# A hybrid decoder step on one core: the first stage in a written order, its x loads on two other queues, and the final norm's sums through a ones matrix

## The chip, the core and the metric

The kernel runs on 1 core of one Trainium2 chip. The core has TensorE (PE in the rows; its weight loads are PEld), VectorE (DVE), ScalarE (ACT), GpSimd (POOL) and SyncE (SP). SP, ACT and POOL also issue DMAs; in the rows an issue stands under SPq, ACTq or POOLq. The metric is the device time of one execution in microseconds (us), as the median over runs.

## The reference

One inference step of one layer over 264 tokens (256 of a prompt, 8 single-token samples), width 2048, all in fp32. RMSNorm comes first, again ahead of the MLP, and once more at the end, where this change touches it:

```python
def rmsnorm(x, g):
    y = x * lax.rsqrt(jnp.mean(x * x, axis=-1, keepdims=True) + EPS)
    return y * g

hx = rmsnorm(x, norm_mix)
proj = hx @ w_in                      # 2048 -> 11264, split into nine parts
...                                   # short convolution branch, gated recurrence branch
x = x + mix @ w_out
h2 = rmsnorm(x, norm_ffn)
x = x + jnp.square(jax.nn.relu(h2 @ w_up)) @ w_down
y = rmsnorm(x, norm_final)
```

## The kernel before

Activations lie transposed: 128 partitions hold one block of 128 features, the free dimension the T = 264 tokens, and a width of 2048 is 16 such blocks (k = 0 to 15). Each product is made of three passes. A weight is split into a rounded part `whi` (a copy on ACT) and the rest `wlo` (a subtraction on DVE), an activation block into `xgh` (ACT, which multiplies by the norm's gain) and `xgl` (DVE), and TensorE adds wh·xh, wh·xl and wl·xh. The factor 1/rms of a norm is applied after the product.

**First stage** (lines 137 to 188). Its output blocks are the four of `HEAD`, accumulated in the four PSUM tiles `hd0` to `hd3`. Weights `w_hd` and input x come in four groups g of four blocks k: `wt0` and `xt0` in four single pieces, the other groups in halves of two blocks (512 KB of weights, 264 KB of x). Per block there are 12 matmuls of 264 columns (line 179). Per group ACT squares the x tile and DVE adds it to `xsq`; after the last group DVE folds that to `ss1` (lines 186 and 187). No order is written here: a scheduler sets each engine's order, and the loads stand in a high-priority block. SP issues weights and x of groups 1 to 3 in turn (lines 155 and 156).

The split tiles come from the pool `wsp` with four buffers a tag, so the ninth `whi` tile takes the buffer of the fifth, and its copy waits until TensorE has used that one. The first stage takes eight such tiles. The next two belong to `w`, the first weight tile of the projection loop (`fetch` and `half`, lines 476 to 482): their first user is `proj`, and their copies wait for the tiles of blocks 8 and 9, and of blocks 10 and 11.

**After it** (lines 484 to 527, in a block whose order is written): `sumsq` puts the squares' sums of 88 tokens at a time on partitions with three matmuls of one column, `rstd_diag` makes 1/rms there (DVE, DVE, ACT, DVE) and `rstd_bcast` spreads it back with one matmul. On TensorE `sumsq(ps1, ss1)` stands between the last `hd` matmul and the first `proj` one.

**The end** (lines 617 to 652). The last norm takes the same way: `sumsq` of `ss3` ahead of the last `dn` product, `sumsq` of the last block's squares behind it, `rstd_diag`, `rstd_bcast`, then DVE multiplies six pieces of the output and SP stores each. Behind `rstd_bcast` stand 48 matmuls of the tile `probe`, whose results nothing reads. At the very start ten matmuls `wps` on a ones tile keep TensorE busy while the first loads run.

Of the kernel before, what the change touches and what calls it, by code (L numbers as in the profile page):

```python
# [40 lines left out]
def hybrid_step(ctx: ExitStack, tc: tile.TileContext, x, par, sconv, shg, w_hd, w_in, w_br, w_out, w_up, w_dn,  # L41
# [115 lines left out]
    for g in range(4):  # L157
        xt, w = xts[g], wts[g]
        whi = [wsp.tile([P, 2, 512], F32R, tag="hi", name="whi") for _ in range(2)]
        wlo = [wsp.tile([P, 2, 512], F32R, tag="lo", name="wlo") for _ in range(2)]  # L160
        for j in range(4):
            k = 4 * g + j
            gk = pt[:, C_NMIX + k:C_NMIX + k + 1]
            hi = act.tile([P, T], F32R, tag="xg", name=f"xgh{k}")
            lo = act.tile([P, T], F32R, tag="xg", name=f"xgl{k}")
            wh, wl = whi[j // 2][:, j % 2], wlo[j // 2][:, j % 2]
            if g == 0:
                (nc.vector.tensor_copy if k == 0 else nc.scalar.copy)(wh, w[:, j])
                nc.scalar.activation(hi, xt[:, j], AF.Copy, scale=gk)
                nc.vector.tensor_tensor(wl, w[:, j], wh.bitcast(F32), op=ALU.subtract)  # L170
            else:
                if j % 2 == 0:
                    split(w[:, j:j + 2], whi[j // 2], wlo[j // 2])
                nc.scalar.activation(hi, xt[:, j], AF.Copy, scale=gk)
            nc.vector.scalar_tensor_tensor(lo, xt[:, j], gk, hi.bitcast(F32), op0=ALU.mult, op1=ALU.subtract)
            xg.append((hi, lo))
            for a, b, st, sp in ((wh, hi, k == 0, False), (wl, hi, False, False), (wh, lo, False, k == NK - 1)):
                for i in range(4):
                    nc.tensor.matmul(hps[i], a[:, i * P:(i + 1) * P], b, start=st, stop=sp)  # L179
        if g == 0:  # L180
            nc.scalar.activation(xsq, xt, AF.Square)
        else:
            sq = xp.tile([P, 4, T], F32, tag="xsq2", name="sq", bufs=2)
            nc.scalar.activation(sq, xt, AF.Square)
            nc.vector.tensor_tensor(xsq, xsq, sq, op=ALU.add)
# [5 lines left out]
    ident = const.tile([P, P], F32, name="ident")
    make_identity(nc, ident)
    cmask = const.tile([P, 2, P], F32, name="cmask")
    nc.gpsimd.memset(cmask, 1.0)
    nc.gpsimd.affine_select(out=cmask, in_=cmask, compare_op=ALU.is_ge, fill=0.0, base=0,
                            pattern=[[0, 2], [1, P]], channel_multiplier=-1)
    nc.gpsimd.memset(cmask[0:CH, :, CH:P], 0.0)
    smask = const.tile([P, 2, TP], F32, name="smask")
    nc.gpsimd.memset(smask, 1.0)
    nc.gpsimd.memset(smask.rearrange("p a (n l) -> p (a n) l", l=CH)[:, :, 0:1], 0.0)  # L200
# [391 lines left out]
    for qd in range(NQ):  # L592
# [17 lines left out]
        for m in range(NK):  # L610
# [15 lines left out]
            else:  # L626
                sumsq(ps3, sq, False, True)
            if m == NK - 2:
                ps3 = mps.tile([P, 512], F32, tag="m", name="ps_rstd3")
                sumsq(ps3, ss3, True, False)  # L630


    with tc.manual_schedule():
# [11 lines left out]
        mv = last_hi[-1]
        row = mv.rearrange("p k c -> p (k c)")
        for n in (512, 128, 256, 264, 280, 320, 384):
            for k in range(6):
                nc.tensor.matmul(probe[:, :n], mv[:, k], row[:, :n], start=True, stop=True)  # L649
        half_w = row.bitcast(BF16)  # L650
        for k in range(6):
            nc.tensor.matmul(probe[:, :T], half_w[:, k * P:(k + 1) * P], half_w[:, :T], start=True, stop=True)
# [55 lines left out]
```

## Time and profile before

| | us |
|---|---|
| median of 3 runs (1501.14 to 1501.60) | 1501.37 |
| the profiled execution, its own time | 1501.61 |
| its span, from the first to the last instruction | 1499.9 |
| PE busy in the span | 1492.7 |
| DVE busy | 884.8 |
| ACT busy | 705.8 |
| first `hd` matmul to first `proj` matmul | 6.40 to 32.93 |
| last `dn` matmul to the span's end | 1486.8 to 1499.9 |

All times of rows are microseconds from the span's start. The span is 1.7 us shorter than its execution's own time. A row of a timeline gives start, length, engine, line, operation and tiles, xcount for merged neighbours, and in brackets how long the engine was idle before and what ended that.

### The profile page before, as it was taken

The page shows a single profiled execution, that of the slowest core. Times are in us where ns is not written, and L with a number is a line of the kernel's source. Part 1 is how long each engine was busy: PE and PEld are TensorE (multiplying, and loading weights), DVE is VectorE, ACT ScalarE, POOL GpSimd, SP SyncE. Part 2 cuts the span into 40 slices and gives each one's busy share as a digit, 9 for nine tenths or more (in the row PEclk, how much of TensorE's full clock was granted, in tenths as well). Part 3 has the DMA queues.
Part 4 walks back from the last instruction along what each step waited for, and adds up shares of the span by engine and source line. Part 5 has one row for each costly group of instructions (what it writes and reads, how often), then busy time and mean ns, then how long its engine had stood idle before and what let it go on. Part 6 is the DMA issues. An engine that isn't in the chain of part 4 may idle for free.

```text
span 1499.9 us, 28243 instructions
## 1 busy us (share of the span) xinstructions
PE 1492.7 (100%) x12230; PEld 1487.2 (99%) x12230; DVE 884.8 (59%) x1154; ACT 705.8 (47%) x946; POOL 57.6 (4%) x86
## 2 busy tenths in 40 slices
PE   9999999999999999999999999999999999999999
PEld 8999999999999999999999999999999999999998
DVE  7576777777655555566655545555455554455554
ACT  6556565646444444444454433444334433344542
POOL 0001011012000000001100000000000000000000
PEclk9999999999999999999999999999999999999999
DMA  6565756665655454555545555454554545545441
GB/s 258 185 256 184 263 189 237 211 241 203 243 176 190 172 192 171 186 202 196 206 170 182 184 172 192 171 186 180 174 192 170 191 173 180 186 171 193 171 169 59
DMA packets 47501, 285.91 MB, mean 191 GB/s; under 512 B 5472, under 2 KB 9328, under 8 KB 16144
## 3 DMA queue, kind: packets, MB, share of 16 engines
q1 hardware_dynamic: 46560, 283.38, 53.0%
q8 instruction: 95, 1.56, 0.4%
q10 hardware_dynamic: 720, 0.59, 0.1%
q14 instruction: 30, 0.25, 0.0%
q0 software_dynamic: 96, 0.14, 0.0%
HBM read 277.07 MB, written 7.02 MB: 189 GB/s over the span
## 4 chain that ended last, share of the span: by engine, by line
PE 98%; DVE 1%; DMA 1%; ACT 0%; issue 0%; ACTq 0%
PE proj L88 11%; PE proj L89 11%; PE proj L90 10%; PE dn L88 8%; PE dn L90 8%; PE up L88 8%; PE dn L89 8%; PE up L89 8%; PE up L90 8%; PE wo L89 2%; PE wo L90 2%; PE wo L88 2%; PE hd L179 1%; PE probe L649 1%; DMA wt<-in_w_hd_dram 0%; PE dlps L332 0%
## 5 line engine op out<-in xcount | busy, mean ns | idle before, releaser
L59 ACT CAST whi<-w 128x1024 fp32r<-128x1024 f32 x488 | 509.5, 1050 | 696.8 <-PE dn L89 218.6
L60 DVE TENSOR_TENSOR wlo<-w,whi 128x1024 fp32r<-128x1024 f32 x488 | 597.8, 1234 | 371.3 <-ACT whi L59 369.5
L88 PE MATMUL proj<-xgh,whi 128*128 128x264 f32 x1344 | 383.5, 285 | 0.4 <-DVE q L462 0.4
L90 PE MATMUL proj<-xgh,wlo 128*128 128x264 f32 x1344 | 381.9, 284 | 0.0
L89 PE MATMUL proj<-xgl,whi 128*128 128x264 f32 x1344 | 380.9, 283 | 0.0
L88 PE MATMUL dn<-hh,whi 128*128 128x264 f32 x1024 | 292.7, 286 | 0.0
L90 PE MATMUL dn<-hh,wlo 128*128 128x264 f32 x1024 | 291.6, 285 | 0.0
L89 PE MATMUL dn<-hl,whi 128*128 128x264 f32 x1024 | 291.4, 285 | 0.0
L89 PE MATMUL up<-x2l,whi 128*128 128x264 f32 x1024 | 291.2, 284 | 0.0
L88 PE MATMUL up<-x2h,whi 128*128 128x264 f32 x1024 | 290.8, 284 | 0.0
L90 PE MATMUL up<-x2h,wlo 128*128 128x264 f32 x1024 | 289.7, 283 | 0.0
L88 PEld LDWEIGHTS proj<-xgh,whi 128*128 128x128 f32 x1344 | 253.4, 189 | 1.7 <-ACT whi L59 0.5
L89 PEld LDWEIGHTS proj<-xgl,whi 128*128 128x128 f32 x1344 | 253.4, 189 | 0.2
L90 PEld LDWEIGHTS proj<-xgh,wlo 128*128 128x128 f32 x1344 | 252.3, 188 | 0.0
L90 PEld LDWEIGHTS dn<-hh,wlo 128*128 128x128 f32 x1024 | 193.5, 189 | 0.0
L90 PEld LDWEIGHTS up<-x2h,wlo 128*128 128x128 f32 x1024 | 193.4, 189 | 0.0
L89 PEld LDWEIGHTS dn<-hl,whi 128*128 128x128 f32 x1024 | 193.4, 189 | 0.0
L88 PEld LDWEIGHTS dn<-hh,whi 128*128 128x128 f32 x1024 | 192.4, 188 | 0.0
L89 PEld LDWEIGHTS up<-x2l,whi 128*128 128x128 f32 x1024 | 192.2, 188 | 0.0
L88 PEld LDWEIGHTS up<-x2h,whi 128*128 128x128 f32 x1024 | 192.1, 188 | 0.0
L90 PE MATMUL wo<-mxh,wlo 128*128 128x264 f32 x256 | 73.0, 285 | 0.0
L89 PE MATMUL wo<-mxl,whi 128*128 128x264 f32 x256 | 72.9, 285 | 0.0
(398 smaller groups left out, 1326.6 us busy)
## 6 DMA issues: line engine op xcount, KB each, us to landing
w<-in_w_in_dram SPq DMA_DIRECT2D x84, 1024.0 KB, 4.8
w<-in_w_up_dram SPq DMA_DIRECT2D x64, 1024.0 KB, 4.8
w<-in_w_dn_dram SPq DMA_DIRECT2D x64, 1024.0 KB, 4.7
w<-in_w_br_dram SPq DMA_DIRECT2D x16, 1024.0 KB, 4.8
w<-in_w_out_dram SPq DMA_DIRECT2D x16, 1024.0 KB, 4.8
so<-in_shg_dram SPq DMA_DIRECT2D x8, 512.0 KB, 7.5
fb<-scr SPq DMA_DIRECT2D x8, 512.0 KB, 8.4
qb<-scr SPq DMA_DIRECT2D x8, 512.0 KB, 10.0
```

Source lines behind the costliest of these rows:

```text
L59: nc.scalar.copy(hi, src)
L60: nc.vector.tensor_tensor(lo, src, hi.bitcast(F32), op=ALU.subtract)
L88: nc.tensor.matmul(ps, wh, xh, start=(k == 0), stop=False)
L89: nc.tensor.matmul(ps, wh, xl, start=False, stop=False)
L90: nc.tensor.matmul(ps, wl, xh, start=False, stop=(k == n - 1))
L179: nc.tensor.matmul(hps[i], a[:, i * P:(i + 1) * P], b, start=st, stop=sp)
L649: nc.tensor.matmul(probe[:, :n], mv[:, k], row[:, :n], start=True, stop=True)
```

## The change

1. Ahead of the first stage: `wps` has 8 matmuls in place of 10; the activation `warm`, which makes ACT load its table of functions, moves behind ACT's second x load.
2. The first stage stands in a written order (`manual_schedule`). Per piece: copy of the weights, `xgh`, `xgl`, `wlo`; TensorE takes wh·xh, wh·xl, wl·xh (before wh·xh, wl·xh, wh·xl). Of block 0 DVE makes `xgh` as well as `whi`. The squares of a group are made one group later, those of the last two groups at the end.
3. The x loads of groups 1 to 3 leave SP's queue for GpSimd's. Two stand ahead of GpSimd's preparation of `ident`, `cmask` and `smask`, four behind.
4. The final norm: one matmul of a 128x128 ones tile with the squares (264 columns) puts the sum on all partitions; ACT takes the square root of all 264 columns from PSUM, DVE the reciprocal of all 264 columns, and the output pieces are multiplied by that tile from SBUF.
5. The `probe` matmuls are gone.

```diff
-    nc.scalar.activation(warm, eps, AF.Sqrt)
     wps = mps.tile([P, 512], F32, tag="m", name="wps")
-    for _ in range(10):
+    for _ in range(8):
...
-    with tc.high_priority():
+    p0_parts = {}
+
+    def p0_split(g, j0, n):
...
+        def cast_x(j):
+            k = 4 * g + j
...
+            if first:
+                nc.vector.tensor_scalar(hi, xts[g][:, j], gk, None, op0=ALU.mult)
+            else:
+                nc.scalar.activation(hi, xts[g][:, j], AF.Copy, scale=gk)
+            nc.vector.scalar_tensor_tensor(lo, xts[g][:, j], gk, hi.bitcast(F32), op0=ALU.mult, op1=ALU.subtract)
+            xg.append((hi, lo))
+
+        (nc.vector.tensor_copy if first else nc.scalar.copy)(whi[:, o:o + n], w)
+        cast_x(j0)
+        nc.vector.tensor_tensor(wlo[:, o:o + n], w, whi[:, o:o + n].bitcast(F32), op=ALU.subtract)
+        for j in range(j0 + 1, j0 + n):
+            cast_x(j)
...
+    with tc.manual_schedule():
         nc.scalar.dma_start(pt, par)
         for j in range(4):
             nc.sync.dma_start(wts[0][:, j:j + 1], w_hd[0][:, j:j + 1])
+            if j < 2:
+                nc.scalar.dma_start(xts[0][:, j:j + 1], x[:, j:j + 1, :])
+        nc.scalar.activation(warm, eps, AF.Sqrt)
+        for j in (2, 3):
             nc.scalar.dma_start(xts[0][:, j:j + 1], x[:, j:j + 1, :])
         for g in range(1, 4):
             for j0 in (0, 2):
                 nc.sync.dma_start(wts[g][:, j0:j0 + 2], w_hd[g][:, j0:j0 + 2])
-                nc.sync.dma_start(xts[g][:, j0:j0 + 2], x[:, 4 * g + j0:4 * g + j0 + 2, :])
...
+                nc.gpsimd.dma_start(xts[g][:, j0:j0 + 2], x[:, 4 * g + j0:4 * g + j0 + 2, :])
+            if g == 1:
+
+                ident = const.tile([P, P], F32, name="ident")
+                make_identity(nc, ident)
...
+            p0_split(0, j, 1)
+            p0_step(j)
+        for g in range(1, 4):
+            for j0 in (0, 2):
+                p0_split(g, j0, 2)
+                for k in (4 * g + j0, 4 * g + j0 + 1):
+                    p0_step(k)
+            p0_squares(g - 1)
+        p0_squares(3)
...
-                sumsq(ps3, sq, False, True)
+                nc.tensor.matmul(ps3, ones, sq, start=False, stop=True)
             if m == NK - 2:
-                ps3 = mps.tile([P, 512], F32, tag="m", name="ps_rstd3")
-                sumsq(ps3, ss3, True, False)
+                ps3 = mps.tile([P, 512], F32, tag="m", name="ps_rstd3")[:, :T]
+                nc.tensor.matmul(ps3, ones, ss3, start=True, stop=False)
...
-        bps = rstd_bcast(rstd_diag(ps3, 2048, "rstd3"), "rstd3")
+
+        bps = const.tile([P, T], F32, name="rstd3")
+        nc.scalar.activation(bps, ps3, AF.Sqrt, scale=1.0 / 2048, bias=eps)
+        nc.vector.reciprocal(bps, bps)
...
-        probe = acc.tile([P, 512], F32, tag="acc", name="probe")
...
```

Three places show what the engines' orders become. First ACT at the end of the first stage, before: `w_471` is the projection's first weight tile, `xgh14` and `xgh15` are the rounded parts of blocks 14 and 15, `sq` are squares.

```order
L59 CAST whi_362<-wt3_112 128x1024
L174 ACTIVATE xgh11_342<-xt2_109,pt_95 128x264
L184 ACTIVATE sq_433<-xt3_111 128x1056
L174 ACTIVATE xgh12_365<-xt3_111,pt_95 128x264
L174 ACTIVATE xgh13_383<-xt3_111,pt_95 128x264
L59 CAST whi_475<-w_471 128x1024
L174 ACTIVATE xgh14_399<-xt3_111,pt_95 128x264
L174 ACTIVATE xgh15_417<-xt3_111,pt_95 128x264
L59 CAST whi_479<-w_471 128x1024
```

The same place now (`w_472` is the projection's tile, `sq_442` and `sq_445` the squares of groups 2 and 3):

```order
L164 ACTIVATE xgh12_373<-xt3_108,pt_92 128x264
L164 ACTIVATE xgh13_378<-xt3_108,pt_92 128x264
L168 CAST whi_406<-wt3_109 128x1024
L58 CAST whi_476<-w_472 128x1024
L58 CAST whi_480<-w_472 128x1024
L164 ACTIVATE xgh14_409<-xt3_108,pt_92 128x264
L164 ACTIVATE xgh15_414<-xt3_108,pt_92 128x264
L187 ACTIVATE sq_442<-xt2_106 128x1056
L187 ACTIVATE sq_445<-xt3_108 128x1056
```

Both copies of the projection's tile now stand ahead of the last two activation blocks, and the squares of the last two groups behind everything.

Second DVE at the end of the first stage, before:

```order
L185 TENSOR_TENSOR xsq_100<-xsq_100,sq_433 128x1056
L175 SCALAR_TENSOR_TENSOR xgl12_366<-xt3_111,pt_95,xgh12_365 128x264
L175 SCALAR_TENSOR_TENSOR xgl13_384<-xt3_111,pt_95,xgh13_383 128x264
L60 TENSOR_TENSOR wlo_476<-w_471,whi_475 128x1024
L186 TENSOR_TENSOR xsq_100<-xsq_100 128x528
L175 SCALAR_TENSOR_TENSOR xgl14_400<-xt3_111,pt_95,xgh14_399 128x264
L175 SCALAR_TENSOR_TENSOR xgl15_418<-xt3_111,pt_95,xgh15_417 128x264
L60 TENSOR_TENSOR wlo_480<-w_471,whi_479 128x1024
L187 TENSOR_TENSOR ss1_96<-xsq_100 128x264
```

And now:

```order
L165 SCALAR_TENSOR_TENSOR xgl14_410<-xt3_108,pt_92,xgh14_409 128x264
L170 TENSOR_TENSOR wlo_407<-wt3_109,whi_406 128x1024
L59 TENSOR_TENSOR wlo_477<-w_472,whi_476 128x1024
L59 TENSOR_TENSOR wlo_481<-w_472,whi_480 128x1024
L165 SCALAR_TENSOR_TENSOR xgl15_415<-xt3_108,pt_92,xgh15_414 128x264
L188 TENSOR_TENSOR xsq_97<-xsq_97,sq_442 128x1056
L188 TENSOR_TENSOR xsq_97<-xsq_97,sq_445 128x1056
L225 TENSOR_TENSOR xsq_97<-xsq_97 128x528
L226 TENSOR_TENSOR ss1_93<-xsq_97 128x264
```

Between `xgl14` and `ss1` stood three large subtractions or folds and `xgl15`; now three subtractions, `xgl15`, two additions of 1056 columns and the fold stand there.

Third GpSimd at the start, before (the preparation of masks, then a load for the convolution branch):

```order
masks.py:197 MEMSET ident_439 128x128
L194 MEMSET cmask_444 128x256
L199 MEMSET smask_448 128x512
masks.py:199 ISA
L213 MEMSET scm0_455 128x256
L213 MEMSET scm1_456 128x256
L215 DMA sc_459<-in_sconv_dram 128x128
```

And now (`xt1` to `xt3` are the x tiles of groups 1 to 3):

```order
L202 DMA xt1_104<-in_x_dram 128x528 x2
masks.py:197 MEMSET ident_126 128x128
masks.py:199 ISA
L208 MEMSET cmask_131 128x256
L213 MEMSET smask_135 128x512
L202 DMA xt2_106<-in_x_dram 128x528 x2
L202 DMA xt3_108<-in_x_dram 128x528 x2
```

Six loads have come to a queue that carried none in the first stage, two of them ahead of all else.

## Rows read from the trace of the kernel before

**Rows 1.** The page's first section (busy time, share of the span, instructions of each engine), and the list of whom PE waited for over the whole span (us in total, times, longest us).

```profile
PE 1492.7 (100%) x12230; PEld 1487.2 (99%) x12230; DVE 884.8 (59%) x1154; ACT 705.8 (47%) x946; POOL 57.6 (4%) x86
...
PE hd L179 <- ACT xgh L169: 2.2, 3, 1.2
PE proj L88 <- DVE q L462: 0.4, 1, 0.4
```

**Rows 2.** Timeline of the first 10 us; L152 is the issue of group 0's x loads, L169 makes `xgh`.

```profile
1.13 4.64 PE L107 MATMUL wps<-ones 128*128 128x128 f32 x20 [1.13 <-DVE eps L102]
...
5.85 0.50 ACT L169 ACTIVATE xgh<-xt,pt 128x264 fp32r<-128x264 f32 x1
...
6.40 0.75 PE L179 MATMUL hd<-xgh,whi 128*128 128x264 f32 x4 [0.63 <-ACT xgh L169]
...
8.72 0.51 ACT L169 ACTIVATE xgh<-xt,pt 128x264 fp32r<-128x264 f32 x1
...
9.28 0.75 PE L179 MATMUL hd<-xgh,whi 128*128 128x264 f32 x4 [1.17 <-ACT xgh L169]
```

**Rows 3.** DMA issues with their number, KB and us from issue to landing: the x loads of block 0 (issued at 1.25) and block 1 (issued at 1.73), and the first half of `wt1` (issued at 4.26).

```profile
xt<-in_x_dram ACTq DMA_DIRECT2D x1, 132.0 KB, 4.5
xt<-in_x_dram ACTq DMA_DIRECT2D x1, 132.0 KB, 5.5
wt<-in_w_hd_dram SPq DMA_DIRECT2D x1, 512.0 KB, 5.6
```

**Rows 4.** Loads and their rate: the stretch 15 to 20 of the first stage (length, then busy time and count of PE, PEld, DVE, ACT, POOL, granted TensorE clock, share of the 16 DMA engines, GB/s); the one load that GpSimd issued near the stage, in its timeline and in the DMA issues; and the queues in the stretch 34.5 to 37 (packets, MB, share), where that load's bytes stand under q0.

```profile
15.00:20.00 5.00, 5.00 (x44) 5.00 (x42) 5.00 (x8) 5.00 (x9) 0.00 (x0) 1.00 1.05 411
...
31.81 0.72 POOL L215 DMA_DIRECT2D sc<-in_sconv_dram  x1
sc<-in_sconv_dram POOLq DMA_DIRECT2D x1, 64.0 KB, 5.6
q0 software_dynamic: 32, 0.07, 6.8%
```

**Rows 5.** Timeline of the end of the first stage, PE first, then ACT and DVE.

```profile
26.70 0.65 PE L179 MATMUL hd<-xgh,whi 128*128 128x264 f32 x4
...
32.03 0.64 PE L179 MATMUL hd<-xgl,whi 128*128 128x264 f32 x4
...
32.93 0.37 PE L88 MATMUL proj<-xgh,whi 128*128 128x264 f32 x1
...
24.42 1.03 ACT L59 CAST whi<-w 128x1024 fp32r<-128x1024 f32 x1
25.36 0.92 ACT L174 ACTIVATE xgh<-xt,pt 128x264 fp32r<-128x264 f32 x2
26.90 1.05 ACT L59 CAST whi<-w 128x1024 fp32r<-128x1024 f32 x1 [0.63 <-PE hd L179]
...
28.72 0.90 DVE L175 SCALAR_TENSOR_TENSOR xgl<-xt,pt,xgh 128x264 fp32r<-128x264 f32 x2
29.53 1.23 DVE L60 TENSOR_TENSOR wlo<-w,whi 128x1024 fp32r<-128x1024 f32 x1
30.67 0.44 DVE L187 TENSOR_TENSOR ss<-xsq 128x264 f32<-128x264 f32 x1
```

**Rows 6.** Groups of the first 45 us by shape (count, busy us, mean ns of one, idle us before): the additions to `xsq` and the fold.

```profile
L185 DVE TENSOR_TENSOR xsq<-xsq,sq 128x1056 f32<-128x1056 f32 x3 | 3.8, 1258 | 0.0
L186 DVE TENSOR_TENSOR xsq<-xsq 128x528 f32<-128x528 f32 x1 | 0.7, 712 | 0.0
```

**Rows 7.** Two stretches of the end on PE alone: length, PE busy and count, granted TensorE clock (1.00 is 2.4 GHz, 0.50 is 1.2 GHz), DMA share, GB/s.

```profile
1486.80:1490.58 3.78, 1.56 (x11) 1.00 0.00 0
1490.58:1493.99 3.41, 3.41 (x13) 0.50 0.50 195
```

**Rows 8.** The end: timeline of PE, DVE and SP's queue, the last piece of the chain of work that ended last (start, us, what), the last store's time to landing, and whom SP waited for from 1495.8 on (us, times, longest).

```profile
1487.78 0.63 PE L114 MATMUL ps_rstd<-ones,sq 128*88 128x1 f32 x6 [0.98 <-ACT sq L621]
...
1489.65 0.68 PE L131 MATMUL bps_rstd<-dg_rstd,ones 88*128 88x264 f32 x2 [1.24 <-DVE dg_rstd L124]
...
1490.37 4.54 DVE L638 TENSOR_TENSOR x2t<-x2t,bps_rstd 128x528 f32<-128x528 f32 x5 [0.87 <-PE bps_rstd L131]
...
1495.40 0.48 SPq L642 DMA_DIRECT2D out_dram<-x2t  x1
...
1498.10 0.69 PE probe L652 x6
...
out_dram<-x2t SPq DMA_DIRECT2D x1, 132.0 KB, 2.9
...
SPq L697 <- DMA out_dram<-x2t: 2.4, 2, 2.0
SPq L697 <- PEq L697: 0.6, 2, 0.5
```

**Rows 9.** Durations (ns, least, median and most, first and last start us, or as in Rows 6): DVE's reciprocals of 8 and of 3 columns, ACT's function of 264 columns read from PSUM, and DVE's operation with a scalar from a tile on 264 columns.

```profile
L519 DVE RECIPROCAL lbm<-lbm x1: 203/203/203, 38.7 to 38.7; 128x8 f32<-128x8 f32 x1
...
L121 DVE RECIPROCAL r_rstd<-r_rstd x3: 171/172/172, 33.3 to 1488.6; 88x3 f32<-88x3 f32 x3
...
L392 ACT ACTIVATE rs<-onps,eps 128x264 f32<-128x264 f32 x8 | 3.4, 477 | 0.0
L236 DVE TENSOR_SCALAR fz<-fz,oml,lb 128x264 f32<-128x264 f32 x8 | 3.0, 412 | 0.0
```

More of the change, by code (lines that the diff above doesn't have):

```diff
@@ L62, in hybrid_step @@
     raws = [wraw]
-    last_hi = []
     def fetch_w(src):
@@ L147, in hybrid_step, with p0_step, p0_squares @@
         wts.append(xp.tile([P, 4, 512], F32, name=f"wt{g}"))
-    with tc.high_priority():
+    p0_parts = {}
+    def p0_split(g, j0, n):
+        if j0 % 2 == 0:
+            p0_parts[g, j0 // 2] = (wsp.tile([P, 2, 512], F32R, tag="hi", name="whi"),
+                                    wsp.tile([P, 2, 512], F32R, tag="lo", name="wlo"))
+        whi, wlo = p0_parts[g, j0 // 2]
+        w, o = wts[g][:, j0:j0 + n], j0 % 2
+        first = g == 0 and j0 == 0
+        def cast_x(j):
+            k = 4 * g + j
+            gk = pt[:, C_NMIX + k:C_NMIX + k + 1]
+            hi = act.tile([P, T], F32R, tag="xg", name=f"xgh{k}")
+            lo = act.tile([P, T], F32R, tag="xg", name=f"xgl{k}")
+            if first:
[9 more added lines that the diff above has]
+            cast_x(j)
+    def p0_step(k):
+        whi, wlo = p0_parts[k // 4, k % 4 // 2]
+        wh, wl = whi[:, k % 2], wlo[:, k % 2]
+        hi, lo = xg[k]
+        for a, b, st, sp in ((wh, hi, k == 0, False), (wh, lo, False, False), (wl, hi, False, k == NK - 1)):
+            for i in range(4):
+                nc.tensor.matmul(hps[i], a[:, i * P:(i + 1) * P], b, start=st, stop=sp)
+    def p0_squares(g):
+        if g == 0:
+            nc.scalar.activation(xsq, xts[g], AF.Square)
+            return
+        sq = xp.tile([P, 4, T], F32, tag="xsq2", name="sq", bufs=2)
+        nc.scalar.activation(sq, xts[g], AF.Square)
+        nc.vector.tensor_tensor(xsq, xsq, sq, op=ALU.add)
+    with tc.manual_schedule():
         nc.scalar.dma_start(pt, par)
@@ L155, in hybrid_step @@
                 nc.sync.dma_start(wts[g][:, j0:j0 + 2], w_hd[g][:, j0:j0 + 2])
-                nc.sync.dma_start(xts[g][:, j0:j0 + 2], x[:, 4 * g + j0:4 * g + j0 + 2, :])
[L157 to L160, printed above, removed]
-        for j in range(4):
[L162 to L185, printed above, removed]
@@ L186, in hybrid_step @@
-    nc.vector.tensor_tensor(xsq[:, 0:2], xsq[:, 0:2], xsq[:, 2:4], op=ALU.add)
-    nc.vector.tensor_tensor(ss1, xsq[:, 0], xsq[:, 1], op=ALU.add)
-    p0.close()
[L191 to L200, printed above, removed]
+                nc.gpsimd.dma_start(xts[g][:, j0:j0 + 2], x[:, 4 * g + j0:4 * g + j0 + 2, :])
+            if g == 1:
+                ident = const.tile([P, P], F32, name="ident")
+                make_identity(nc, ident)
+                cmask = const.tile([P, 2, P], F32, name="cmask")
+                nc.gpsimd.memset(cmask, 1.0)
+                nc.gpsimd.affine_select(out=cmask, in_=cmask, compare_op=ALU.is_ge, fill=0.0, base=0,
+                                        pattern=[[0, 2], [1, P]], channel_multiplier=-1)
+                nc.gpsimd.memset(cmask[0:CH, :, CH:P], 0.0)
+                smask = const.tile([P, 2, TP], F32, name="smask")
+                nc.gpsimd.memset(smask, 1.0)
+                nc.gpsimd.memset(smask.rearrange("p a (n l) -> p (a n) l", l=CH)[:, :, 0:1], 0.0)
@@ L203, in hybrid_step @@
+        for j in range(4):
+            p0_split(0, j, 1)
[7 more added lines that the diff above has]
+        p0_squares(3)
+        nc.vector.tensor_tensor(xsq[:, 0:2], xsq[:, 0:2], xsq[:, 2:4], op=ALU.add)
+        nc.vector.tensor_tensor(ss1, xsq[:, 0], xsq[:, 1], op=ALU.add)
+    p0.close()
     rstd1 = const.tile([P, T], F32, name="rstd1")
@@ L642, in hybrid_step @@
         nc.sync.dma_start(y[:, 15:16, :], x2t[3][:, 3:4])
-        probe = acc.tile([P, 512], F32, tag="acc", name="probe")
[L645 to L652, printed above, removed]
 _OUTS = [(P, NK, T), (P, NC_, 2), (NH, P, P), (P, NC_, TS, 2), (NH, P, TS, P)]
```

2 lines of the change are left out of this document (removed).

## The prediction

> **What bounds the kernel now.** I read the page's first section, then the list of whom PE waited for: PE is busy for all but a few us, and of the waits ahead of the end only 2.2 us in the first stage and 0.4 us behind it count [rows 1]. So a change to the first stage is worth what it does to the start of `proj`, at 32.93 [rows 5]; behind that PE has nothing to wait for, and a shift there goes through to the end one to one. The end is a second, separate place: from 1486.8 on a chain of single steps runs, and there every step counts.
>
> In the first stage the reader is to see two things. `hd` starts at 6.40, when ACT has made `xgh` of block 0, and then stands still for 1.17 us ahead of block 1, whose `xgh` ACT makes only at 8.72 [rows 2], though its x has been there since 1.73 + 5.5 = 7.2 [rows 3]: ACT took three weight copies first. Then the matmuls run without a gap. From 26.70 to 32.03 there are 11 groups of four, 0.485 us each; a block is 1.454 us, and 26.70 is the start of block 12 [rows 5]. In what follows T is that moment. Before, `proj` starts at T + 6.23, and `ss1` is done at 30.67 + 0.44 = 31.1, 1.4 us ahead of its use [rows 5].
>
> **The start of the first stage.** Table load and x arrive together before: x of block 0 lands at 1.25 + 4.5 = 5.75 [rows 3], ACT works on it from 5.85 [rows 2]. So moving the table load gives 0.1 us by itself. On DVE `xgh` takes some 0.41 us [rows 9] in place of ACT's 0.5; with 0.05 us on either side `hd` would start at 6.25. The written order lets ACT make `xgh` of block 1 as soon as its x is there: 7.2 + 0.05 + 0.51 makes 7.8, just behind block 0's end at 6.25 + 1.45 = 7.7. If nothing else changed, T would be 7.8 + 11 x 1.454 = 23.8, that is 2.9 us earlier than 26.70. That is the change's best case.
>
> Against it stands the move of the x loads. GpSimd's issue takes 0.72 us, and its load's bytes move in the stretch from 34.5 on, 2.7 us behind the issue [rows 4]; so the two loads at the head of its queue move from about 3.5 on, amid the pieces of group 0. The DMA engines are full (411 GB/s at a share of 1.05 [rows 4]), and 2 x 264 KB = 0.54 MB takes 1.3 us of them. Block 0 has half of that ahead of it, block 1 all: `hd` starts at 6.25 + 0.65 = 6.9, and `xgh` of block 1 is there at 7.8 + 1.3, about 9.2 with rounding to the next matmul, so T = 9.2 + 11 x 1.454 = 25.2. The other bound: all six x loads (1.62 MB, 3.95 us at 411 GB/s) come ahead of the first half of `wt1`, which landed at 4.26 + 5.6 = 9.86 [rows 3]; then it lands at 13.8, copy and `xgh` of block 4 end 0.94 + 0.51 + 0.1 later [rows 2, 5], and T = 15.35 + 8 x 1.454 = 27.0. I take 25.2, since four of the six loads are issued behind the masks' preparation. The Trainium skill (DMA: Bandwidth & Descriptors, "Issuing engines are not separate DMA queues") speaks against this part of the change: loads of all queues interleave on the same 16 engines, and a second issuer saves only issue time. By that rule the move gains nothing, and the trace agrees in that a share of 1.05 leaves nothing to share out. SP keeps only weight issues; its queue waited for landings, not for issuing, and gains nothing on PE's path.
>
> **The end of the first stage.** Here the order rows decide. ACT's second copy of the projection's tile waits for PE to be through with blocks 10 and 11: before, ACT sat idle 0.63 us for PE and started at 26.90, T + 0.20 [rows 5]. Now `whi` is done with one group of matmuls earlier (the order of the three passes), so the copy starts at T - 0.29. Queued behind it on ACT are both last activation blocks and the squares of two groups. From there: copies stand 0.94 apart (24.42 to 25.36 [rows 5]), so `xgh14` is done at T + 0.65 + 0.51 = T + 1.16. DVE takes `xgl14` at T + 1.2 (0.41 to the next, from 0.90 for two), then three subtractions 1.14 apart (29.53 to 30.67 [rows 5]), so `xgl15` runs from T + 5.03 to T + 5.52. PE needs it at T + 4.85 and waits **0.7 us**; `hd` ends at T + 6.52. DVE goes on from T + 5.44: two additions of 1.26, the fold of 0.71 [rows 6], `ss1` of 0.44 [rows 5], each 0.03 behind the other: `ss1` is done at T + 9.2. `sumsq` waits for it, **2.7 us**, and lasts 0.42 (32.03 + 0.485 to 32.93 [rows 5]): `proj` starts at T + 9.67, 3.44 us later against T than before. With T = 25.2 that is 34.87, **1.9 us later than 32.93**; by the bounds for T, 0.5 to 3.7 later. The sums of the norm, which had 1.4 us to spare, are what is late next; nothing hides them, since PE's next instruction is `sumsq`. What is behind `proj`'s start (the 1/rms chain, the 0.4 us wait) keeps its distance.
>
> **The clock.** From T + 4.85 to T + 9.67 PE has only two groups of matmuls and the one-column sums. At the end of the kernel before, PE worked 1.56 of 3.78 us, and after that the granted clock was 0.50 for 3.41 us [rows 7], 1.2 in place of 2.4 GHz. Here PE works about 1.4 of 4.8 us, so I expect the same fall. A stretch of 3.41 us at half the clock costs 1.7 us if all of it lies in matmuls; part of it will lie in the wait, and the 0.4 us wait behind `proj` disappears into it. I take 0.9, with bounds 0 and 1.7. At the start the shorter warm-up (16 records in place of 20, so 3.7 us by [rows 2]) leaves PE idle from 4.85 to 6.9; a fall there would hit blocks 0 and 1, which wait for x anyway, so I put it at nothing; uncovered it costs up to 1.7.
>
> **The end of the kernel.** Before, from the start of the last `sumsq` at 1487.78 to the first output product at 1490.37 it is 2.59 us [rows 8]. Now: one matmul of 264 columns in fp32 (0.68, as L131 [rows 8]), ACT's root of 264 columns from PSUM (0.48 [rows 9]), the reciprocal, and 0.04 us between steps. The trace has reciprocals of 3 and 8 columns alone, 172 and 203 ns [rows 9], 6.2 ns a column; for 264 columns an estimate of 0.17 + 261 x 0.0062 = 1.8 us. Its lower bound is DVE's ordinary 0.43 to 0.49 us for 264 columns [rows 5]. Sum: 0.68 + 0.48 + 1.8 + 0.1 = 3.06, 0.5 later. I take the slope, since both rows are reciprocals. The Trainium skill (VectorE: DVE Perf Modes, "First, the fixed hardware budget") has the reciprocal as an iterative divide with a repeat count of 8. At its 8 cycles of 0.96 GHz, 264 columns would be an estimate of 2.2 us, and the sum 0.4 us more. The slope, 6 cycles a column, agrees in kind. The products from SBUF cost what they cost from PSUM.
>
> The `probe` matmuls: the last store is issued at 1495.40 and lands 2.9 later, at 1498.3; SP waits for it, then another 0.5 for PE [rows 8], whose probe ends at 1498.10 + 0.69 = 1498.79. So removing 48 matmuls is worth 0.5 us and not their 8, since the store is next. 0.5 later, 0.5 saved: **0** (bounds -1.3 with a short reciprocal, +0.4). The one matmul ahead of the last `dn` product takes about as long as the six records that it replaces.
>
> **Sum.** 1.9 + 0.9 + 0 = 2.8 us. The profiled execution took 1501.61 and would take 1504.4; against the median 1501.37, which I forecast, it is 1504.2. A measurement of this kernel can tell about 0.2% (3.0 us) from no change, so this is within it, close to its upper edge.
>
> **The rivals.**
> - The sums are late but the clock stays up: 1501.37 + 1.9 = 1503.3. For it: the fall hangs on where the idle time lies. Chance 0.22 against 0.45 for the forecast.
> - Slower: GpSimd's loads crowd out the weights of group 1. At the bound T = 27.0, `proj` starts at 36.7, and with the clock's 0.9 the time is 1506.0; from T = 25.3 on it is slower by over 0.2%. For it: two of the loads stand ahead of everything in their queue, and the other four follow within some 4 us. Against it: six loads are no more bytes than before, and group 1's weights have slack. Chance 0.18.
> - The reciprocal is as quick as other operations of 264 columns: -1.3, so 1502.9. Against it the two rows of reciprocals. Chance 0.10.
> - The order does what it says: `xgh14`, `xgl15` and the sums come in time, T = 23.8, `proj` at 30.0, and 1501.37 - 2.9 = 1498.5. The order rows speak against it: nine DVE operations stand between PE's release and `ss1`. Chance 0.05.
>
> **How the numbers follow.** The forecast's own spread (T from 24.6 to 25.8, clock 0 to 1.7) is 1503 to 1505.3; 0.6 of it lies within 0.2%, so 0.27 same and 0.18 slower. The second case is 0.21 same, 0.01 slower; crowding 0.03 and 0.15; the reciprocal 0.10 same; the order as it says 0.03 faster, 0.02 same. Together 0.03 faster, 0.63 same, 0.34 slower. The range 1501.8 to 1506.0 leaves out the last case and the ends of the others.
>
> **What would show it.** In the profile of the changed kernel: `hd` starting at 6.3 to 7.0; block 1 at 7.8 to 9.2; ahead of the second group of block 15 a wait for `xgl15`; ahead of `sumsq` a wait of 2 to 3 us for `ss1`, the longest of the stage; `proj` starting at 34 to 36; a granted clock of 0.50 somewhere between 31 and 39; one reciprocal of 1.6 to 2.3 us; the last store landing near 1498.8 plus the shift, PE long done. The forecast is wrong if `ss1` is ready when `hd` ends, if `proj` starts before 32.9, or if the reciprocal takes under 0.6 us.

## The result and the profile after

The changed kernel is slower. Against 1501.48 us for the kernel before, four executions took 1509.67, 1509.59, 1509.41 and 1507.49 us: median 1509.5, ratio 1.0050, 95% interval 1.0033 to 1.0068. Five more gave 1507.85 in the median, ratio 1.0045 (1.0031 to 1.0059). The forecast was 1504.2, with a range up to 1506.0: the sign of its sum was right, its size was not (2.8 us in place of 8.0 and 6.3). The profiled execution took 1509.67, of which 1508.0 is the span; before, the span was 1499.88, so 8.1 us are to be found.

The page's first section after, and the list of whom PE waited for in the first 60 us (us in total, times, longest). They answer to [rows 1]:

```profile
PE 1487.8 (99%) x12168; PEld 1482.3 (98%) x12168; DVE 886.8 (59%) x1153; ACT 705.6 (47%) x945; POOL 60.8 (4%) x92
```

```profile
PE ps L110 <- DVE ss L226: 2.5, 1, 2.5
PE hd L180 <- ACT xgh L164: 1.7, 3, 1.0
...
PE hd L180 <- DVE xgh L162: 0.8, 1, 0.8
PE hd L180 <- DVE xgl L165: 0.6, 1, 0.6
PE proj L85 <- DVE q L489: 0.4, 1, 0.4
```

The wait for `ss1`, which did not exist before, is the longest. Those for ACT's `xgh` should have shrunk and didn't: behind block 0 they are 1.7 us, and before they were 1.6 (2.2 less the 0.63 ahead of block 0 [rows 2]).

**The start of the stage**, timeline of PE, then of ACT (start, us, what, and in brackets the idle time before and what ended it), for [rows 2]:

```profile
5.70 1.25 PE L180 MATMUL hd<-xgh,whi 128*128 128x264 f32 x4 [0.79 <-DVE xgh L162]
6.75 1.08 PE L180 MATMUL hd<-xgl,whi 128*128 128x264 f32 x4
7.63 1.08 PE L180 MATMUL hd<-xgh,wlo 128*128 128x264 f32 x4
9.21 0.81 PE L180 MATMUL hd<-xgh,whi 128*128 128x264 f32 x4 [0.50 <-ACT xgh L164]
...
14.21 0.75 PE L180 MATMUL hd<-xgh,whi 128*128 128x264 f32 x4 [1.03 <-ACT xgh L164]
...
8.65 0.51 ACT L164 ACTIVATE xgh<-xt,pt 128x264 fp32r<-128x264 f32 x1 [3.03 <-DMA xt<-in_x_dram]
...
13.64 0.51 ACT L164 ACTIVATE xgh<-xt,pt 128x264 fp32r<-128x264 f32 x1 [1.89 <-DMA xt<-in_x_dram]
```

`hd` starts 0.7 us earlier than before, but its first groups stand 1.05 and 0.88 us apart; before it was 0.59 and 0.48, so block 0 ran at about half pace. (So early the trace has no record of the clock, and views print 1.00; the warm-up's matmuls go at 0.236 us a record here, those of the same form in run 6 below at 0.12.) Then ACT waits for x, 3.03 us ahead of block 1 and 1.89 ahead of block 3, and PE waits behind it. Block 1 starts at 9.21, where the forecast had it (9.2). T, the start of block 12, is 28.08; before it was 26.70. From block 1 to T it is 18.9 us, and eleven blocks without a wait would take 16.0.

A part of what held x up stands in the stretch 5 to 7 us (length, busy time of PE, PEld, DVE, ACT, POOL, clock, DMA share, GB/s), first of the kernel before, then of the changed one, and in the queues of the changed one (packets, MB, share):

```profile
5.00:7.00 2.00, 1.37 (x9) 1.07 (x9) 0.84 (x3) 1.85 (x4) 0.00 (x0) 1.00 1.02 355
```

```profile
5.00:7.00 2.00, 1.30 (x6) 1.30 (x7) 1.46 (x3) 0.61 (x1) 1.90 (x4) 1.00 0.95 264
```

```profile
q1 hardware_dynamic: 110, 0.21, 41.9%
q0 software_dynamic: 68, 0.21, 33.4%
q10 hardware_dynamic: 106, 0.11, 20.1%
```

q1 is SP's queue, q10 ACT's, with x of group 0, and q0 GpSimd's. The engines are busy to 0.95 and move a quarter less; 0.21 MB of that is x of group 1, which nobody needs yet. Runs 8 and 10 below show the other part.

**The end of the stage** (PE, ACT, DVE), for [rows 5]:

```profile
28.08 0.64 PE L180 MATMUL hd<-xgh,whi 128*128 128x264 f32 x4
...
33.70 0.75 PE L180 MATMUL hd<-xgl,whi 128*128 128x264 f32 x4 [0.56 <-DVE xgl L165]
...
37.43 1.04 PE L110 MATMUL ps<-ones,ss 128*88 128x1 f32 x6 [2.50 <-DVE ss L226]
38.33 0.57 PE L85 MATMUL proj<-xgh,whi 128*128 128x264 f32 x1
...
27.84 1.05 ACT L58 CAST whi<-w 128x1024 fp32r<-128x1024 f32 x1 [1.03 <-issue]
28.79 0.92 ACT L164 ACTIVATE xgh<-xt,pt 128x264 fp32r<-128x264 f32 x2
...
30.88 2.35 DVE L59 TENSOR_TENSOR wlo<-w,whi 128x1024 fp32r<-128x1024 f32 x2
33.15 0.49 DVE L165 SCALAR_TENSOR_TENSOR xgl<-xt,pt,xgh 128x264 fp32r<-128x264 f32 x1
33.56 2.61 DVE L188 TENSOR_TENSOR xsq<-xsq,sq 128x1056 f32<-128x1056 f32 x2
36.20 0.71 DVE L225 TENSOR_TENSOR xsq<-xsq 128x528 f32<-128x528 f32 x1
36.95 0.43 DVE L226 TENSOR_TENSOR ss<-xsq 128x264 f32<-128x264 f32 x1
```

`ss1` is done at 37.38, T + 9.30, and `proj` starts at T + 10.25 (before T + 6.23). **The clock** behind it, stretches with the columns as above, for [rows 7]:

```profile
33.00:36.66 3.66, 1.37 (x10) 1.03 (x8) 3.52 (x5) 0.00 (x0) 0.00 (x0) 1.00 0.65 206
36.66:43.48 6.82, 6.05 (x29) 6.05 (x30) 4.12 (x10) 2.09 (x3) 1.18 (x5) 0.50 0.18 60
43.48:50.00 6.52, 6.16 (x49) 5.91 (x48) 3.67 (x11) 3.86 (x5) 0.00 (x0) 1.00 0.45 157
```

PE worked 1.37 of 3.66 us, and for the next 6.82 us the granted clock was 0.50 (1.2 in place of 2.4 GHz): `sumsq` and nearly all of the first `proj` product ran at it.

**The end**, timeline, for [rows 8] and [rows 9]:

```profile
1495.51 0.71 PE L654 MATMUL ps_rstd<-sq,ones 128*128 128x264 f32 x2 [0.97 <-ACT sq L648]
1496.26 0.48 ACT L663 ACTIVATE rstd<-ps_rstd,eps 128x264 f32<-128x264 f32 x1 [0.80 <-PE ps_rstd L654]
1496.77 1.80 DVE L664 RECIPROCAL rstd<-rstd 128x264 f32<-128x264 f32 x1 [1.77 <-ACT rstd L663]
1498.61 4.56 DVE L668 TENSOR_TENSOR x2t<-x2t,rstd 128x528 f32<-128x528 f32 x5
```

From the sums to the first output product it is 3.10 us, before 2.59. The reciprocal takes 1.80 us, as estimated from the rows of 3 and 8 columns; the longer estimate of 2.2 was not reached.

So the span's 8.1 us are T +1.4, the way from T to `proj` +4.0, the first `proj` product +2.3 (9.19 us to the start of the second in place of 6.86), and the end +0.4 (13.40 us from the last `dn` addition in place of 13.04).

### The profile page after: what moved, and what is told of

Same layout as the page of the kernel before. It is cut to its first block, busy times and chain, and to the rows that moved or that the text cites. A ratio compares the mean times of both kernels' runs of the same rounds, so it can differ in the third digit from the quotient of the medians.

```text
span 1508.0 us, 28125 instructions
## 1 busy us (share of the span) xinstructions
PE 1487.8 (99%) x12168; PEld 1482.3 (98%) x12168; DVE 886.8 (59%) x1153; ACT 705.6 (47%) x945; POOL 60.8 (4%) x92
## 4 chain that ended last, share of the span: by engine, by line
PE 96%; DVE 2%; DMA 1%; ACT 0%; issue 0%; DVEq 0%; ACTq 0%
PE proj L85 11%; PE proj L86 11%; PE proj L87 10%; PE dn L85 8%; PE dn L87 8%; PE dn L86 8%; PE up L85 8%; PE up L86 8%; PE up L87 8%; PE wo L86 2%; PE wo L87 2%; PE wo L85 2%; PE hd L180 1%; DMA xt<-in_x_dram 1%; DVE wlo L59 0%
```

## The experiments

All are built from the changed kernel, except where said. Fillers apart, none adds or leaves out work of the reference.

**1. x loads back on SP.**

```diff
-                nc.gpsimd.dma_start(xts[g][:, j0:j0 + 2], ...)
+                nc.sync.dma_start(xts[g][:, j0:j0 + 2], ...)
```

> The x loads of groups 1 to 3 are issued by SP again, alternating with the weights, as in the kernel before; all else is the changed kernel. Theory (GpSimd's loads move early and in larger packets, and push back the pieces of group 0): x of blocks 1 and 2 lands at about 7 us and not at 8.6 and 10.7, block 3 does not wait 1.0 us for x, T (the start of block 12) is about 25.2 in place of 28.1, the late sums and the low clock behind them stay as they are: about 1506.6 us, 2.9 less than the changed kernel. Rival (the loads don't matter, block 0 at half the clock sets the start of block 1 and what follows): T stays at 27.5 to 28.1 and the time at 1509.0 to 1509.5.

Measured 1500.94 (1500.46 to 1501.08), 8.6 us less than the changed kernel and three times what the theory gave. T is 24.25, as expected, but the sums were no longer late:

```profile
PE hd L180 <- DVE xgh L162: 1.1, 1, 1.1
PE ps L110 <- DVE ss L226: 0.9, 1, 0.9
```

The order had moved with the loads. The copies of the projection's tile belong to the next written section, and the scheduler, which sets their place among the first section's instructions, put them behind `xgh14`, `xgh15` and the squares once x came from SP. So this run mixes two things; 2, 5 and 14 part them.

**2. The sums in time**, loads on GpSimd as in the changed kernel. The fetch and the copies of the projection's tile move into the first section:

```diff
+SQ = {(1, 2): (0,), (2, 0): (1,), (3, 0): (2, 3)}
...
+        for i in range(2):
+            fetch(i)
         for g in range(1, 4):
...
-            p0_squares(g - 1)
-        p0_squares(3)
+                if (g, j0) in SQ:
+                    for q in SQ[g, j0]:
+                        p0_squares(q)
...
+        half(0, 0)
+        half(0, 1)
     p0.close()
```

> Only the place of the projection's tile and of the squares in the written order is changed: the squares go between the blocks, and the copies and subtractions of the projection's tile come behind ss1; the loads stay as in the changed kernel. Theory (the sums are late because nine VectorE operations stand ahead of ss1, and the fall of the clock follows from the waits that this brings): no wait of PE for xgl15, at most 0.3 us for ss1, the granted clock stays up behind hd, proj starts at T + 6.3 to T + 7.0 in place of T + 10.4: about 1503.2 us, 6.3 less. Rival 1 (the clock falls whatever the waits are): the clock is at 0.50 for some us behind hd, about 1506.0. Rival 2 (the sums are not what is late, the 1/rms chain is): the wait comes back ahead of the first use of the 1/rms product, about 1508.

1502.55 (1501.79 to 1503.34); the profiled execution took 1503.30. T is 28.18, `sumsq` has no wait, `proj` starts at T + 6.29, and the granted clock is 1.00 from there on. That is the theory; both rivals fall.

**3. Ten warm-up matmuls** (`range(8)` to `range(10)`).

> Ten warm-up matmuls in place of eight, all else the changed kernel. Theory (block 0 runs at half the clock because PE stood still longer ahead of it; but the x of blocks 1 to 3 is what sets T): the clock is up at 5.8 to 6.0, block 0 takes 2.0 us in place of 3.5, PE then waits some 1.5 us longer for xgh of block 1, T and the time stay: 1509.2 to 1509.5 us. Rival 1 (the low clock of block 0 holds back everything behind it): T is 1 to 1.8 us earlier, 1507.7 to 1508.5 us. Rival 2 (the rise hangs on something else than the warm-up's length): the clock is still 0.50 until about 9.35.

1508.67 (1507.09 to 1509.54), between the two medians of the changed kernel. Block 0 ran at full pace, and PE then waited 1.2 us for block 1. T is 26.89, but run 4, with eight warm-ups and a block 0 at half pace, has 27.03. ACT starts on x of block 3 at 12.43 and 12.65 in these two, and at 13.64 in the changed kernel: T follows that, not the number of warm-ups. Nor does it set block 0's pace: a second trace of the changed kernel has it fast with eight, run 7 slow with ten.

**4. The final norm of before, without the probe.** `sumsq`, `rstd_diag` and `rstd_bcast` come back at the end.

> The final norm is that of the kernel before (one-column sums, 1/rms of three columns, product with a diagonal), without the probe matmuls; the first stage is that of the changed kernel. Theory (the reciprocal of 264 columns makes the new form 0.5 us longer than the old): from the last sums to the first output product 2.6 us in place of 3.1, about 1509.0 us, 0.5 less. Rival (the ones matrix makes up for it): the chain is as long as or longer than the new one, 1509.5 to 1509.9 us.

1508.19 (1506.81 to 1508.68). From the sums to the first product it is 3.13 us, as long as the new form, though the same steps took 2.59 before. The product with the diagonal ran at half the clock:

```profile
1495.13 1.22 PE L127 MATMUL bps_rstd<-dg_rstd,ones 88*128 88x264 f32 x2 [1.24 <-DVE dg_rstd L120]
```

Before it took 0.68 [rows 8], and run 11 has 0.68 too; run 7, with this form of the norm, has 1.22 again. So which form is quicker hangs on whether the clock has fallen by then. What decides that is not shown: the two traces with 0.68 have the first stage of before, the two with 1.22 the new one or run 2's.

**5. Loads on SP, sums late.** The order on PE, VectorE and ScalarE is held word for word as in the changed kernel, by writing the copies of the projection's tile ahead of `cast_x(14)` and its subtractions ahead of `cast_x(15)`'s.

> The x loads go back to SP, but the order of the instructions on PE, VectorE and ScalarE is held word for word as in the changed kernel (in the run with the loads on SP alone the order had moved with them). Theory (two separate costs, the loads' 3.8 us and the late sums' 3.5 us with the fall of the clock behind them): T about 24.3, ss1 done at T + 9.3, PE waits 2.5 us ahead of sumsq, the clock falls, proj starts at T + 10.3 = 34.6 and the time is about 1505.4 us. Rival (the loads on SP do all of the gain of 8.6 us, the order is of no matter): about 1501 us. Rival 2 (the order does it all): about 1509 us.

1506.95 (1506.05 to 1507.64). T is 24.89, the waits are back, and the clock is at 0.50 for 6.83 us:

```profile
PE ps L110 <- DVE ss L253: 2.5, 1, 2.5
...
PE hd L191 <- DVE xgl L165: 0.8, 1, 0.8
```

The time is 1.5 us above the theory's, T 0.6. So the late sums cost as much without GpSimd's loads, and both rivals fall: neither the loads nor the order do it all.

**6. Fillers in the wait.** Nine unused matmuls stand between `hd` and `sumsq`.

```diff
+        fps = mps.tile([P, 512], F32, tag="m", name="fps")
+        for _ in range(9):
+            nc.tensor.matmul(fps[:, :P], ones, ones, start=True, stop=True)
     p0.close()
```

> The changed kernel with nine matmuls of the warm-up's form (ones by ones, 128 columns, their result unused) between the last hd matmul and sumsq, inside the wait of 2.5 us for ss1. Theory (PE's standing still is what the fall of the clock follows): the granted clock stays at 1.0 behind hd, sumsq takes 0.45 us in place of 0.9, the first proj product runs at 0.12 us a matmul throughout, and the start of the second product comes 2.8 us earlier against T: about 1506.7 us by the changed kernel's median. Rival 1 (the fall comes whatever PE does there): 1509.3 us. Rival 2 (the fillers themselves delay sumsq): 1508 us.

1506.08 (1505.53 to 1506.54). The sums are as late (`sumsq` at T + 9.36), and the clock stays up, here from 36.5 to 43.5:

```profile
33.81 2.17 PE L229 MATMUL fps<-ones 128*128 128x128 f32 x18
36.47 0.63 PE L110 MATMUL ps<-ones,ss 128*88 128x1 f32 x6 [0.49 <-DVE ss L226]
```

```profile
36.50:43.50 7.00, 6.96 (x56) 6.68 (x56) 4.30 (x13) 4.96 (x8) 1.18 (x5) 1.00 0.23 56
```

The first product takes 6.87 us again. The fall follows from PE standing still, and is a cost of its own: 1.8 to 3.4 us by the two medians of the changed kernel, which have the spread of T in them, and 1.6 to 2.7 us in `sumsq` and the first product of its two traces.

**7. A combined version:** loads on SP, sums in time, ten warm-ups, the old final norm, no probe.

> The x loads on SP, the projection's tile and the squares placed so that ss1 is early, ten warm-up matmuls, the final norm of the kernel before and no probe. Theory: T about 24.0 to 24.3, no wait ahead of sumsq, proj at T + 6.3 = 30.5, that is 2.4 us ahead of the kernel before; the end chain 0 to 0.5 us shorter than that kernel's with its probe: about 1498.8 us. Rival (the 1/rms chain or the copies of the next tiles come late instead): 1500 to 1501 us.

1499.58 (1499.01 to 1501.14), ratio to the kernel before 0.9986 (0.9977 to 0.9994): faster than the changed kernel by over 8 us, and than the kernel before by 0.14%, a small difference that the interval just clears. The profiled execution was the slowest of the eleven; block 0 ran at half pace in it and T is 25.60. `proj` starts at T + 6.29. The final norm's product took 1.22 us, so nothing came of the 0.5 us hoped for there.

**8 and 10. Half of the loads each.** In 8 the loads of group 1 go to SP and the rest stays on GpSimd (order held as in the changed kernel); 10 is run 2 with groups 2 and 3 on SP.

> Only the two x loads of group 1, which stand at the head of GpSimd's queue, go back to SP; groups 2 and 3 stay on GpSimd, and the order on PE, VectorE and ScalarE is held as in the changed kernel. Theory (it is the head of GpSimd's queue that collides with group 0): blocks 1 to 3 no longer wait for x, T is 24.3 to 25.0, the sums stay late: 1505.4 to 1506.2 us. Rival (the loads of groups 2 and 3 push back the weights of group 1 just as much): T 26 to 28, 1507.5 to 1509.5 us.

> The run with the sums in time again, with the x loads of groups 2 and 3 back on SP, alternating with their weights; the two of group 1 stay at the head of GpSimd's queue. Theory (both halves of the loads cost about the same, as the run with only group 1 on SP gave about half back): T 26 to 27, 1501.2 to 1502.2 us. Rival 1 (the head of the queue does most): T 27.5 to 28.5, 1502.5 us. Rival 2 (only the later loads matter): T 24.3 to 25, about 1500 us.

8 gives T = 26.14 and 1507.09 (1506.45 to 1507.91), 10 gives T = 26.26 and 1501.48 (1501.05 to 1503.11). The seven traces with all six loads on GpSimd and two of them ahead have T from 26.89 to 28.18, so T comes earlier with either half: neither the head of the queue nor the later loads carry it alone. In 8 (first row) group 0 is undisturbed from 5 to 7 us and block 3 waits 1.5 us later; in 10 (second row) GB/s are low in that stretch although POOL itself stands still:

```profile
5.00:7.00 2.00, 1.20 (x9) 1.15 (x9) 1.45 (x3) 0.79 (x2) 0.44 (x1) 1.00 1.04 358
```

```profile
5.00:7.00 2.00, 1.37 (x6) 1.37 (x7) 1.45 (x3) 0.57 (x1) 0.07 (x1) 1.00 0.93 268
```

What T hangs on is x of block 3, the last piece of group 0. ACT starts on it, in 8, in 10, and in 14 with all loads on SP, at:

```profile
11.63 0.51 ACT L164 ACTIVATE xgh<-xt,pt 128x264 fp32r<-128x264 f32 x1 [2.64 <-DMA xt<-in_x_dram]
...
11.84 0.52 ACT L165 ACTIVATE xgh<-xt,pt 128x264 fp32r<-128x264 f32 x1 [0.80 <-DMA xt<-in_x_dram]
...
9.96 0.52 ACT L165 ACTIVATE xgh<-xt,pt 128x264 fp32r<-128x264 f32 x1 [0.74 <-DMA xt<-in_x_dram]
```

With all loads on GpSimd it is 13.75 in run 2 (12.43 to 13.75 in the seven traces). So against 9.96 the later four cost 1.7 us, the first two 1.9, and all six 3.8: the two halves nearly add. Behind this piece ACT makes the next copy and `xgh` of block 4, and DVE the `wlo` that the third pass of block 4 needs. T is ACT's start on it plus 14.4 to 14.6 us in twelve of the fifteen traces with the written order; in 7 and 12 PE came to that pass later by itself, and in 13 the clock fell behind it. The later four loads cost at full rate. From 7 to 9 us the engines moved 413 GB/s in 8, and ACT's queue got half of what it got in 14 (8 first, then 14):

```profile
q0 software_dynamic: 115, 0.42, 51.8%
q10 hardware_dynamic: 72, 0.07, 9.7%
...
q10 hardware_dynamic: 136, 0.13, 19.8%
```

**9. Smaller GpSimd loads.** Run 2 with twelve loads of one block in place of six of two.

> The run with the sums in time again (x loads on GpSimd), with each of GpSimd's six x loads of two blocks issued as two loads of one block. Theory (GpSimd's queue takes the share that it does because its packets are 4224 bytes against 1056 for the pieces of group 0): smaller packets, a smaller share, the pieces of group 0 land earlier, T 25.5 to 27 in place of 28.2, 1500.5 to 1501.8 us. Rival (the share hangs on something else, or the twelve issues come later and cost as much): T 27 to 29, 1502 to 1503.5 us.

1502.24 (1502.07 to 1502.91), T = 27.07, both in the rival's range. It doesn't decide: the packets were 4224 bytes again (384 of them, as with six loads), so the size that was to be changed was not.

**11. The kernel before without its probe.**

> The kernel before without its 48 probe matmuls at the end, nothing else. Theory (the last store lands 0.5 us ahead of the probe's end): 0.4 to 0.5 us less, 1500.9 to 1501.2 us. Rival (what PE does there keeps the clock up for the final norm's product, and without it that product takes twice as long): 1501.3 to 1501.6 us.

1501.49 (1501.04 to 1502.53) beside 1501.55 on the same chip. The end is 13.04 us behind the last `dn` addition, as with the probe, and SP waits for the same:

```profile
SPq L687 <- DMA out_dram<-x2t: 2.4, 2, 2.0
SPq L687 <- PEq L687: 0.6, 2, 0.5
```

The 0.5 us at PE's queue stands at the end of the program whether PE has work or not. The theory falls; so does the rival, since the diagonal's product took 0.68 here too.

**The changed kernel again.**

> The changed kernel again, on the chip of the three others, for its spread and for a second trace of it. Theory (when the x pieces of group 0 land differs from execution to execution by 1 us, and the length of the low clock by one step of 3.41 us): 1507 to 1509.7 us, T between 26.9 and 28.2. Rival (the first four executions were an exception): below 1506.

1507.85 (1507.59 to 1509.30). The nine executions fall into two groups, 1507.49 to 1507.85 and 1509.26 to 1509.67; the mean granted clock over the span is 0.996 in the first and 0.993 to 0.995 in the second. The first profile is of the upper group; this one, of the lower, has the low clock for half as long, and T = 27.62:

```profile
38.50:41.91 3.41, 3.41 (x18) 3.41 (x17) 2.94 (x6) 1.64 (x2) 0.00 (x0) 0.50 0.08 22
```

**12 and 13. Early x by another queue, and GpSimd's loads later.** Both are run 2. In 12 SP issues x of group 1 ahead of everything and groups 2 and 3 with their weights; in 13 GpSimd's six loads stand behind the masks.

> The run with the sums in time, with no x load on GpSimd: SP issues the two x loads of group 1 ahead of everything else, those of groups 2 and 3 alternate with their weights. Theory (it is GpSimd's queue that crowds out group 0, not that x of group 1 moves early): between 5 and 7 us the engines move 340 GB/s or more, and blocks 1 to 3 do not wait for x once block 0 has begun; block 0 itself begins about 0.7 us later, as the weights are issued later; T 25 to 26, 1500.0 to 1501.3 us. Rival (early bytes of group 1 crowd out group 0 from any queue): 264 to 290 GB/s between 5 and 7 us, T 26.5 to 28.2, 1501.5 to 1503 us.

> The run with the sums in time, with all six of GpSimd's x loads behind its preparation of the masks. Theory (only loads that move before group 0 is in cost it; later ones collide with its last two pieces as in the run with group 1 on SP): 340 GB/s or more between 5 and 7 us, blocks 1 and 2 without a wait for x, a wait of about 1 us at block 3 or 4, T 26 to 27, 1501 to 1502 us. Rival (GpSimd's loads cost the same wherever they stand): T 27.5 to 28.2, 1502.5 us.

12: 361 GB/s from 5 to 7 us, no wait for x once block 0 has begun, at 7.28. T is 26.24 and the time 1501.89 (1501.17 to 1503.41), in the rival's range, since block 0 began later than thought and ran at half pace. So it is not x moving early that slows the engines down. Moving it early costs time even so: by the medians 12 is 1.8 us above 14, in which SP issues x of group 1 in its turn. 13: 336 GB/s, blocks 1 and 2 on time, then a wait of 2.0 us at block 3 and the clock at 0.50 for 3.41 us; T = 28.47, 1502.26 (1501.54 to 1503.73). This profiled execution is the slowest of the eleven, and the fall of the clock is in its T. The waits moved as the theory has it, the median is nearer the rival's: the loads cost about the same, only later.

**14. The fourth corner:** run 2 with all x loads on SP.

> The run with the sums in time with all x loads on SP, the order on PE, VectorE and ScalarE the same. Theory (the two costs add): T 24.2 to 24.9, no wait ahead of sumsq, proj at 30.6 to 31.2, 1499.3 to 1500.0 us, that is 2.5 to 3.2 us less than with the loads on GpSimd. Rival (the weights of group 1, later behind the x loads on SP, become the bound): T above 25.5, 1501 us.

1500.08 (1499.63 to 1500.87), ratio 0.9988 (0.9979 to 0.9997); T = 24.37, `proj` at T + 6.29. By the medians the two costs add, if the first of the changed kernel is taken:

| median us | sums late | sums in time |
|---|---|---|
| x from GpSimd | 1509.5 and 1507.85 | 1502.55 |
| x from SP | 1506.95 | 1500.08 |

The loads are worth 2.6 us with the sums late and 2.5 with them in time, the sums 7.0 and 6.9. With the second median of the changed kernel, 1507.85, the loads are worth 0.9 with the sums late and the sums 5.3, so how well they add is known to about 1.7 us.

## Why the prediction was wrong

| term, us against before | forecast | profiled | second trace |
|---|---|---|---|
| T | -1.5 | +1.4 | +0.9 |
| from T to `proj` | +3.4 | +4.0 | +3.6 |
| first `proj` product | +0.9 (all of the clock) | +2.3 | +1.6 |
| end | 0 | +0.4 | +0.4 |

(Of the second trace's 6.5 us, 0.2 are made up again behind the first product; its span is 6.2 us longer.)

**The step that failed is T**, in "The start of the first stage": "T = 9.2 + 11 x 1.454 = 25.2", with "I take 25.2, since four of the six loads are issued behind the masks' preparation". The price of the first two loads for block 1, 1.3 us, was about right: block 1 starts at 9.21 (8.87 in the second trace). What was wrong is the step behind it, that nothing waits from there on. The sum has no term for x of blocks 2 and 3, and the four later loads cost nothing in it. x of block 3 came only at 13.64, and from block 1 to T it was 18.9 us in place of 16.0. Run 8 shows the later four by themselves, 10 and 14 what is left without them.

The rows of before warned of that step: they do not show that "the matmuls run without a gap". 9.28 + 16.0 makes 25.3, and T was 26.70; and of the 2.2 us of waits for `xgh` in [rows 1] the two shown in [rows 2] make only 1.8.

The bytes were priced at 411 GB/s. That also failed for a while: from 5 to 7 us the engines moved 264 GB/s, with x from SP 344 to 375, and ACT's pieces of group 0 got 0.11 MB in place of 0.24 (run 1). With the same order on both sides T is 28.18 from GpSimd and 24.37 from SP (2 and 14): 3.8 us, of which 3.4 are in the times of these two executions; by the medians the loads cost 2.5. The best case of the working, T = 23.8, was nearly right for SP (24.25 to 24.89 in runs 1, 5 and 14); against the kernel before the written order gains 2.3 us at the start (14). The rival "GpSimd's loads crowd out the weights of group 1" had the engine right and the victim wrong: blocks 1 to 3 wait for x of group 0. Its bound T = 27.0 was passed in both traces of the changed kernel.

The Trainium skill's rule (DMA: Bandwidth & Descriptors, "Issuing engines are not separate DMA queues"), by which a second issuer saves only issue time, was right that there is nothing to gain. The runs go beyond it: here a second issuer lost, 2.5 us by the medians of 2 and 14.

**The late sums were forecast rightly.** `ss1` at T + 9.2 was T + 9.30, the wait of 0.7 us 0.56, that of 2.7 us 2.50; run 2 removes both. (Before, only `xgl15` and one subtraction stood between `xgl14` and `ss1` in the order shown under "The change", not three large operations.) Not foreseen was that the late sums come from the same line of the diff: with the loads on SP the scheduler put the copies elsewhere (run 1).

**The clock was forecast in kind and mis-sized:** 0.9 with an upper bound of 1.7, taken from one stretch of 3.41 us. It was 6.82 us in one trace and 3.41 in the other: 2.7 us in all in the profiled one (2.3 in the product, 0.4 in `sumsq`), 1.6 in the second. Run 6 shows it by itself. At the start, "I put it at nothing" held only as long as x was late anyway (3 and 4). With x from SP, block 0 at half pace goes with a T of 25.60 (7) where 14 has 24.37: block 1 starts 1.24 us later, and PE does not wait behind it. That rests on one execution of each.

**The end:** the chain's 0.5 and the reciprocal's 1.8 us were right. The 0.5 us for the probe was not: the wait of SP for PE was put down to the probe's last matmul because the two ended at about the same time (11). From the issue of the last store to the end it is 4.31 us in place of 4.48, so that 0.4 of the reciprocal's 0.5 are left.

The rivals of a quick reciprocal (it took 1.80 us) and of a clock that stays up did not come about, nor did an order that does what it says.

Open is why the engines move less from 5 to 7 us with GpSimd's first two loads, and why its queue gets so large a share later. For the first, x moving early is ruled out (12), POOL's work on the masks too (10). The larger packets, 4224 bytes against 1056 on ACT's queue, fit both, but the run that was to change them did not, so that cause is not shown.

## What to carry to other kernels

A load that is moved to another queue is to be costed at what the loads beside it get while it moves, not at its bytes: compare GB/s and MB per queue of the same stretch, and follow it to the last piece that the stage waits for, not the first. Where a scheduler merges sections, a move of loads can reorder the compute engines too; read the order again with the loads alone put back before giving a cost to either. A wait on PE in front of dense work can cost its own length and then the low clock behind it, here 1.6 to 2.7 us on top of 3.1 us of waiting.

## What the runs showed of the hardware that was not expected

The same kernel kept the low clock for 6.83 us in one traced execution and for 3.41 in the other, and its times fall into two groups 1.4 to 2.2 us apart. Whether block 0 starts at half pace differs between the two traces of the changed kernel. The DMA engines can be busy to 0.90 to 0.97 and, from 5 to 7 us, move only 264 to 309 GB/s, in every trace with x of group 1 at the head of GpSimd's queue, against 336 to 375 in all others. At a full 413 GB/s, GpSimd's queue moved 0.42 MB in 2 us and ACT's 0.07, where without GpSimd's loads ACT's moved 0.13 (8 and 14). The end of the program holds a wait of SP of 0.5 us at PE's queue, with 48 matmuls of PE there and without them (before and 11).
